# The gated merge of a hybrid decoder layer: from SBUF tiles to the PSUM banks of the products

## The chip, the cores and the metric

The kernel runs on one core of one Trainium2 chip. A core has five engines that work beside each other, each through its own queue in order: TensorE (PE in the profile, with its weight loads as PEld), VectorE (DVE), ScalarE (ACT), GpSimd (POOL) and SyncE (SP, which here issues most of the DMAs). They wait for each other by semaphores. Matrix products are written into PSUM, a small memory of eight banks; everything else lies in SBUF. The metric is the device time of one execution in microseconds (us), as the median of several runs. An execution with the hardware profiler gives the trace.

## The reference, cut to what matters

One inference step of a decoder layer for 512 prompt tokens and 8 x 4 decode tokens, 544 tokens in all, in fp32. Two attention branches run on the same normalised input: branch A, a sparse attention over the 256 best keys, and branch B, a stick-breaking attention. Each branch's output (512 wide) is projected to 1024 channels, the two are merged by sigmoid gates, and an output projection and a residual follow, then a SwiGLU FFN:

```python
gates = jax.nn.sigmoid(p[7]).reshape(b, t, 2, D_MODEL)
...
merged = gates[:, :, 0] * (o_a @ w_br_a) + gates[:, :, 1] * (o_b @ w_br_b)
return merged @ w_o
...
hp = hp + _mixers(...)
hp = hp + _ffn(_rmsnorm(hp, norm_ffn[layer]), w_ffn_gate[layer], w_ffn_up[layer], w_ffn_down[layer])
```

## The kernel before

Everything is computed transposed: channels lie on the 128 partitions, the 544 tokens along the free axis. A token axis is worked in two halves of 256 and 288 tokens (`halves`), because a PSUM bank holds 512 fp32 numbers per partition. A product of 1024 output channels is eight blocks m of 128 channels.

To keep fp32 accuracy in a faster number format (fp32r), every operand is split into a high and a low part, and a product is the sum of three matmuls (high weight by high data, low by high, high by low). The weights' parts are made on the way: class `Weights` loads a block by DMA from SP (`wst`, line 106), ACT copies the high part (`wh`, line 116), and POOL subtracts to get the low part in two instructions (`wl`, line 119). `W.take()` hands out the next block and prepares the blocks ahead. The inner loop of all such products is `pieces` (line 464): for each half it takes the next PSUM bank of a cycle and runs 3 matmuls for each of the nk slices of 128 input channels.

The banks have names: `mm` and `z` (one bank each), `acc`, `tp` and `ts` (two each), together eight. From here on the products go round the four banks `mm, z, acc, acc` (`banks`, line 454), one pair for each block m. The two `ts` banks serve the attention; after it nothing uses them until the FFN opens a new PSUM pool.

The place of the change is the merge, lines 1395 to 1411, between attention and output projection:

- `hT` (SBUF) holds the products of branch B. Five blocks were computed earlier and come back by DMA from DRAM (line 1402); the last three are computed here (lines 1396 to 1400).
- For each block m, two gate tiles `t` and `g` (tag `gt`, 8 buffers) are loaded by SP (line 1391) and put through a sigmoid by ACT (line 1392). POOL multiplies g into `hT` (line 1405).
- PE computes the block of branch A, 12 matmuls for each half (nk is 4). For each half DVE multiplies the bank by the gate t into SBUF (line 1407), adds `hT` (line 1408), ACT copies the result as the high part `mh` (line 1409), and DVE subtracts to get the low part `ml` (line 1410). `mh` and `ml` are the input of the output projection with `w_o`, eight blocks of 2 x 24 matmuls, whose results get the residual from transposed pieces of x (`xe`, line 1425, transposed by PE at line 414).

The instructions of each engine's queue are not in the order of the code. The framework schedules them by its own model of time over the whole program, so an edit in one place can move instructions elsewhere; it also puts in the semaphores, and lets a buffer be written again when its last reader is done.

Of the kernel before, what the change touches and what calls it, by code (L numbers as in the profile page):

```python
# [15 lines left out]
AF = mybir.ActivationFunctionType  # L16
# [245 lines left out]
def hybrid_step(ctx: ExitStack, tc: tile.TileContext, x_prompt, x_sample, cache_kv_a, cache_k_idx, cache_kv_b,  # L262
                page_table, w_in, w_br_a, w_br_b, w_o, norm_attn, norm_ffn, w_gate, w_up, w_down, norm_final,
                c_ident, c_rope, c_masks, y_p, y_s, kva_p, kidx_p, kvb_p, kva_s, kidx_s, kvb_s):
    nc = tc.nc
    S = lambda t: t.bitcast(F32)

    def opened(name, bufs=1, **kw):
        st = ExitStack()
        return st.enter_context(tc.tile_pool(name=name, bufs=bufs, reuse_waits="tile", **kw)), st  # L270
# [113 lines left out]
        nc.gpsimd.indirect_dma_start(out=dst, out_offset=None, in_=src,  # L384
                                     in_offset=bass.IndirectOffsetOnAxis(ap=rowid[:, n:n + 1], axis=0))

    V = {"wide": True}
    V["psum"], psum_end = opened("pmm", space=PSUM)

    def bank(tag, bufs):  # L390
        return V["psum"].tile([P, 512], F32, tag=tag, name=tag, bufs=bufs)

    mm = lambda: bank("mm", 1)
    zb = lambda: bank("z", 1)
    acc = lambda: bank("acc", 2)
    lat = lambda: bank("tp", 2)
    lts = lambda: bank("ts", 2)
# [7 lines left out]
    halves = [slice(0, 2 * P), slice(2 * P, TOK)]  # L405
# [45 lines left out]
    nc.vector.tensor_scalar(rowid, prow[:, :NSEQ], masks[:, 2 * P + 3 * NS:2 * P + 3 * NS + 1], None, op0=OP.add)  # L451
    xp_end.close()

    banks = cycle([mm, zb, acc, acc])


    def pieces(w, a, nk, m=P):

        (wh, wl), (ah, al) = w, a
        for f, hs in enumerate(halves):  # L460
            ps = (next(banks) if V["wide"] else mm)()[:m, :hs.stop - hs.start]
            for k in range(nk):
                for p, (ww, aa) in enumerate(((wh, ah), (wl, ah), (wh, al))):
                    nc.tensor.matmul(ps, ww[:, k, :m], aa[:, k, hs],  # L464
                                     start=(k == 0 and p == 0), stop=(k == nk - 1 and p == 2))
                yield None
            yield hs, ps

    def product(w, a, nk, m=P):
        return (part for part in pieces(w, a, nk, m) if part)  # L470
# [19 lines left out]
    def row(name, shape=(P, TOK), dt=F32):  # L490

        pool, bufs = V.get("rows", (rp if name == "y" else rr, (2, 2, 2, 1)))
        return pool.tile(list(shape), dt, tag="row" + name, name="row" + name, bufs=bufs["ywhl".index(name)])
# [10 lines left out]
    def rope(m=P, scale=1.0, also=None):  # L504
# [12 lines left out]
        nc.vector.tensor_mul(y[:m], y[:m], cosT[:m])  # L517
        (nc.vector if V["wide"] else nc.gpsimd).tensor_mul(w[:m], w[:m], sinT[:m])
        nc.vector.tensor_add(y[:m], y[:m], w[:m])
# [115 lines left out]
    def dense_idx():  # L635
        ip = V["ip"]
        qs, qbi, kinew, khh, kll, wiT, wtok, wrow = V["idx"]
# [652 lines left out]
    def branch_product(b):  # L1290
        return product(W.take(), place(b), 4)
# [77 lines left out]
    rp_end.close()  # L1369
    wk_end.close()  # L1370

    V["wide"] = True

    late, late_end = opened("late")
    hT = late.tile([P, KD, TOK], F32, name="hT")
# [8 lines left out]
    mh = ep.tile([P, KD, TOK], F32R, name="mh")  # L1384
    ml = ep.tile([P, KD, TOK], F32R, name="ml")
# [3 lines left out]
    def gate(m, b):  # L1389
        t = gp.tile([P, TOK], F32, tag="gt", name="gt", bufs=8)  # L1390
        nc.sync.dma_start(t, gate_d[:, 2 * m + b, :])
        nc.scalar.activation(t, t, AF.Sigmoid)
        return t
# [9 lines left out]
    for m in range(KD):  # L1403
        t, g = gate(m, 0), gate(m, 1)
        nc.gpsimd.tensor_mul(hT[:, m, :], g, hT[:, m, :])
        for hs, ps in branch_product(0):
            nc.vector.tensor_mul(t[:, hs], ps, t[:, hs])  # L1407
            nc.vector.tensor_add(t[:, hs], t[:, hs], hT[:, m, hs])
            nc.scalar.activation(mh[:, m, hs], t[:, hs], AF.Copy)
            nc.vector.tensor_sub(ml[:, m, hs], t[:, hs], S(mh[:, m, hs]))  # L1410
    W.extra, W.ahead = None, 1
    gp_end.close()
    xk_end.close()
# [41 lines left out]
    for hs in hv:  # L1455
        ps = lat()[:, :HN]
# [61 lines left out]
    x_parts("T4", t4)  # L1518
    psum_end.close()
    V["psum"], psum_end = opened("pff", space=PSUM)  # L1520
    tp2_end.close()
    xu_end.close()
    hp_end.close()
# [16 lines left out]
    for j in range(1, KF // 2):  # L1540
        banks2, kept = {}, {}
        for name in Pairs.REST if j > 1 else Pairs.FIRST:
# [4 lines left out]
            ps = banks2[b][:, :, :HN]  # L1547
# [107 lines left out]
                nc.sync.dma_start(y_s.rearrange("n t d -> (n t) d"), yt[:NS, i, :])  # L1655

    for m in range(KD):
        pss = [next(banks)()[:, :hs.stop - hs.start] for hs in halves]
        for ks in DOWN[0]:
            w = W.take()  # L1660
            for f, hs in enumerate(halves):
                down(pss[f], w, ks, hs)
        for f, hs in enumerate(halves):
            nc.vector.tensor_add(hT[:, m, hs], pss[f], hT[:, m, hs])
    act_parts(KF)
    for m in range(KD):
        pss = [next(banks)()[:, :hs.stop - hs.start] for hs in halves]
        if m < KD - 1:
            for ks in DOWN[1]:
                w = W.take()  # L1670
                for f in range(2):
                    down(pss[f], w, ks, halves[f])
            for f in range(2):
                rows_of(m, f, pss[f])
        else:
            ws = [W.take(), W.take()]
            for w, ks in zip(ws, DOWN[1]):
                down(pss[1], w, ks, halves[1])
            down(pss[0], ws[0], DOWN[1][0], halves[0])
            rows_done(1, rows_of(m, 1, pss[1]))  # L1680
            down(pss[0], ws[1], DOWN[1][1], halves[0])
            rows_done(0, rows_of(m, 0, pss[0]))
# [32 lines left out]
```

## Time and profile before

| | us |
|---|---|
| median of 3 runs | 1070.34 (1068.96 to 1074.01) |
| the profiled execution | 1067.42 |
| its span, first to last instruction | 1065.6 |

| engine | busy share of the span |
|---|---|
| PE | 92% |
| DVE | 70% |
| ACT | 50% |
| POOL | 44% |

The profile page gives shares over the whole span. The kernel has stages with different limits, so the page is only a start: the trace is asked for windows of time (busy time of each engine in each), for the instructions of one engine in order of time, and for groups of like instructions. In the windows table the numbers after each engine are its busy microseconds and, in brackets, its instructions; then come the granted TensorE clock as a share of full speed, the share of time that the DMA engines were busy, and GB/s. Matmuls overlap: one is shown as 0.28 us long, and the next starts 0.12 us after it.

### The profile page before, as it was taken

How to read it: one execution, taken by the hardware profiler on the slowest of the kernel's cores; microseconds unless marked ns; L12 is line 12 of the kernel's file. 1: busy time of each engine (PE TensorE's matmuls, PEld its weight loads, DVE VectorE, ACT ScalarE, POOL GpSimd, SP SyncE). 2: the span in 40 equal slices, each digit the busy share in tenths (PEclk: the TensorE clock that was granted, in tenths of full speed). 3: DMA queues.
4: the chain of work that ended last, by engine and by line, in shares of the span. 5: the costliest groups of instructions: out<-in, count | busy, mean ns of one | idle time of the engine just before them, and what ended most of it. 6: DMA issues, size and time to landing. Idle time of an engine off the chain costs nothing.

```text
span 1065.6 us, 20642 instructions
## 1 busy us (share of the span) xinstructions
PE 984.7 (92%) x7446; PEld 931.0 (87%) x7446; DVE 740.7 (70%) x1441; ACT 531.2 (50%) x1020; POOL 469.9 (44%) x413
## 2 busy tenths in 40 slices
PE   6899998787989996999999799979999999999995
PEld 5899998776669996888888799979999999999995
DVE  4468995798997786578784976787787876513233
ACT  6234535574556564677785544534444444423223
POOL 4555545226763236652635834411323232545441
PEclk9999999998999998999998999989999999999998
DMA  9775547886767765864525663223432341223222
GB/s 269 181 205 169 152 121 228 250 253 174 228 209 242 223 188 165 256 218 144 193 72 181 201 179 90 71 71 89 119 100 83 97 119 43 75 88 90 83 82 85
DMA packets 184704, 162.15 MB, mean 152 GB/s; under 512 B 13338, under 2 KB 148058, under 8 KB 183578
## 3 DMA queue, kind: packets, MB, share of 16 engines
q1 hardware_dynamic: 176410, 140.00, 45.5%
q0 software_dynamic: 1872, 10.75, 2.9%
q10 hardware_dynamic: 6320, 10.08, 2.9%
q8 instruction: 59, 0.97, 0.4%
q14 instruction: 43, 0.35, 0.1%
HBM read 133.37 MB, written 22.01 MB: 146 GB/s over the span
## 4 chain that ended last, share of the span: by engine, by line
PE 52%; DVE 11%; issue 7%; POOL 5%; DMA 4%; ACT 2%; SPq 1%; ACTq 0%; DVEq 0%; POOLq 0%
PE mm L464 8%; PE ffB L1553 8%; PE acc L1607 6%; PE ffC L1553 5%; PE ffA L1553 5%; POOL wl L119 4%; PE z L1607 3%; PE mm L1607 3%; PE acc L1021 2%; PE ts L992 2%; PE acc L1089 2%; DVE g L909 1%; DMA vb<-in_cache_kv_b 1%; PE tp L825 1%; PE tp L838 1%
## 5 line engine op out<-in xcount | busy, mean ns | idle before, releaser
L119 POOL TENSOR_TENSOR wl<-wst,wh 128x512 fp32r<-128x512 f32 (+2 forms) x198 | 228.8, 1177 | 193.8 <-ACT wh L116 193.8
L464 PE MATMUL mm<-xh,wh 128*128 128x256 f32 (+2 forms) x484 | 145.7, 301 | 9.3 <-ACT rowy L500 5.5
L464 PE MATMUL mm<-xh,wl 128*128 128x256 f32 (+2 forms) x484 | 141.6, 293 | 2.4 <-POOL wl L119 2.4
L464 PE MATMUL mm<-xl,wh 128*128 128x256 f32 (+2 forms) x484 | 142.5, 294 | 0.0
L116 ACT ACTIVATE wh<-wst 128x1024 fp32r<-128x1024 f32 (+3 forms) x99 | 88.6, 895 | 103.0 <-PE z L1607 42.1
L227 POOL TENSOR_TENSOR wl<-wst,wh 128x512 fp32r<-128x512 f32 x40 | 59.9, 1519 | 164.4 <-ACT wh L224 164.4
L464 PEld LDWEIGHTS mm<-xh,wh 128*128 128x128 f32 (+1 forms) x484 | 93.1, 192 | 21.0 <-issue 7.3
L464 PEld LDWEIGHTS mm<-xh,wl 128*128 128x128 f32 (+1 forms) x484 | 93.1, 192 | 3.4 <-POOL wl L119 2.6
L464 PEld LDWEIGHTS mm<-xl,wh 128*128 128x128 f32 (+1 forms) x484 | 93.0, 192 | 0.5
L224 ACT ACTIVATE wh<-ws 128x1024 fp32r<-128x1024 f32 x40 | 42.4, 1061 | 68.5 <-PE ffC L1553 36.1
L1607 PE MATMUL acc<-actp,wh 128*128 128x256 f32 (+1 forms) x352 | 68.1, 289 | 0.0
L910 POOL TENSOR_TENSOR b<-b,g 128x127 f32<-128x127 f32 (+3 forms) x32 | 28.4, 887 | 82.8 <-DVE g L909 43.0
L229 DVE TENSOR_TENSOR wl<-ws,wh 128x1024 fp32r<-128x1024 f32 x40 | 52.1, 1301 | 6.0 <-ACT wh L224 6.0
L1607 PEld LDWEIGHTS acc<-actp,wh 128*128 128x128 f32 x352 | 55.4, 188 | 0.1
L998 DVE TENSOR_TENSOR kl<-ts,kh 128x512 fp32r<-128x512 f32 x64 | 43.4, 686 | 16.2 <-ACT kh L997 15.5
L464 PE MATMUL acc<-xh,wh 128*128 128x256 f32 (+1 forms) x176 | 51.3, 293 | 3.1 <-DVE gt L1407 2.7
L464 PE MATMUL acc<-xh,wl 128*128 128x288 f32 (+1 forms) x176 | 51.4, 293 | 0.0
L464 PE MATMUL acc<-xl,wh 128*128 128x288 f32 (+1 forms) x176 | 51.0, 291 | 0.0
L1607 PE MATMUL acc<-actp,wl 128*128 128x256 f32 (+1 forms) x176 | 49.9, 288 | 1.2 <-POOL wl L119 1.2
L997 ACT ACTIVATE kh<-ts 128x512 fp32r<-128x512 f32 x64 | 38.0, 602 | 23.9 <-PE ts L992 20.1
L1083 POOL TENSOR_TENSOR vl<-vb,vh 128x512 fp32r<-128x512 f32 x24 | 36.6, 1529 | 28.0 <-ACT vh L1082 24.9
L1082 ACT ACTIVATE vh<-vb 128x512 fp32r<-128x512 f32 x64 | 38.4, 626 | 20.6 <-DMA vb<-in_cache_kv_b 13.0
(438 smaller groups left out, 3433.7 us busy)
## 6 DMA issues: line engine op xcount, KB each, us to landing
wst<-in_w_in SPq DMA_DIRECT2D x38, 512.0 KB, 4.3
kb<-in_cache_kv_b SPq DMA_DIRECT2D x64, 256.0 KB, 4.6
vb<-in_cache_kv_b SPq DMA_DIRECT2D x64, 256.0 KB, 4.0
wst<-in_w_ffn_gate SPq DMA_DIRECT2D x40, 256.0 KB, 3.0
wst<-in_w_ffn_up SPq DMA_DIRECT2D x40, 256.0 KB, 3.4
wst<-in_w_ffn_down SPq DMA_DIRECT2D x16, 384.0 KB, 3.6
wst<-in_w_ffn_down SPq DMA_DIRECT2D x16, 320.0 KB, 3.2
gate_d<-rowy ACTq DMA_DIRECT2D x16, 272.0 KB, 4.2
```

Of the source, the lines that this page charges most:

```text
L116: self.nc.scalar.activation(h, st, AF.Copy)
L119: self.nc.gpsimd.tensor_sub(l[:, k], st[:, k], h[:, k].bitcast(F32))
L224: self.nc.scalar.activation(h, src, AF.Copy)
L227: self.nc.gpsimd.tensor_sub(l[:, g], src[:, g], h[:, g].bitcast(F32))
L229: self.nc.vector.tensor_sub(l, src, h.bitcast(F32))
L464: nc.tensor.matmul(ps, ww[:, k, :m], aa[:, k, hs], start=(k == 0 and p == 0), stop=(k == nk - 1 and p == 2))
L997: nc.scalar.activation(kh[:, :, :2 * P], tpv, AF.Copy)
L998: nc.vector.tensor_sub(kl[:, :, :2 * P], tpv, S(kh[:, :, :2 * P]))
L1082: nc.scalar.activation(vh, raw, AF.Copy)
L1083: (nc.vector if pg % 3 else nc.gpsimd).tensor_sub(vl, raw, S(vh))
L1553: nc.tensor.matmul(ps[:, g], ww[:, g, k, :], aa[:, k, :], start=(first and k == 0 and p == 0), stop=(k == 3 and p == 2), skip_group_check= ...
L1607: nc.tensor.matmul(ps, ww[:, k - ks[0], :], aa[:, hs], start=(k in (DOWN[0][0][0], DOWN[1][0][0]) and p == 0), stop=(k + 1 in (DOWN[0][1][ ...
```

## The change

The merge of a half is done in the PSUM bank that its product stands in. Line 1407 multiplies the bank by t and writes the bank, line 1408 adds `hT` to the bank and writes the bank, line 1409 reads the high part from the bank and line 1410 the low part. The gate tile t is only read. A bank is therefore held until line 1410 has read it, where before it was free after line 1407.

From the merge on, the products go round six banks, `mm, z, acc, acc, ts, ts`. The cycle now lies in `V["banks"]`; it is set back to the four banks when the FFN's PSUM pool opens.

```diff
-    V = {"wide": True}
+    V = {"wide": True, "banks": cycle([])}
...
-    banks = cycle([mm, zb, acc, acc])
+    V["banks"], many = cycle([mm, zb, acc, acc]), cycle([mm, zb, acc, acc, lts, lts])
...
-            ps = (next(banks) if V["wide"] else mm)()[:m, :hs.stop - hs.start]
+            ps = (next(V["banks"]) if V["wide"] else mm)()[:m, :hs.stop - hs.start]
...
-    V["wide"] = True
+    V["wide"], V["banks"] = True, many
...
         nc.gpsimd.tensor_mul(hT[:, m, :], g, hT[:, m, :])
         for hs, ps in branch_product(0):
-            nc.vector.tensor_mul(t[:, hs], ps, t[:, hs])
-            nc.vector.tensor_add(t[:, hs], t[:, hs], hT[:, m, hs])
-            nc.scalar.activation(mh[:, m, hs], t[:, hs], AF.Copy)
-            nc.vector.tensor_sub(ml[:, m, hs], t[:, hs], S(mh[:, m, hs]))
+            nc.vector.tensor_mul(ps, ps, t[:, hs])
+            nc.vector.tensor_add(ps, ps, hT[:, m, hs])
+            nc.scalar.activation(mh[:, m, hs], ps, AF.Copy)
+            nc.vector.tensor_sub(ml[:, m, hs], ps, S(mh[:, m, hs]))
...
     V["psum"], psum_end = opened("pff", space=PSUM)
+    V["banks"] = cycle([mm, zb, acc, acc])
...
-        pss = [next(banks)()[:, :hs.stop - hs.start] for hs in halves]
+        pss = [next(V["banks"])()[:, :hs.stop - hs.start] for hs in halves]
```

The schedule moves with it. DVE's queue near the end of the merge, before: the instructions on block 6 (banks `mm` and `z`) stand between those of the blocks beside it.

```order
L1407 TENSOR_TENSOR gt<-mm,gt 128x256
L1410 TENSOR_TENSOR ml<-gt,mh 128x256
L1407 TENSOR_TENSOR gt<-z,gt 128x288
L1410 TENSOR_TENSOR ml<-gt,mh 128x288
L1408 TENSOR_TENSOR gt<-gt,hT 128x256
L1408 TENSOR_TENSOR gt<-gt,hT 128x288
L1410 TENSOR_TENSOR ml<-gt,mh 128x256
```

The two rows of line 1410 that stand between the two multiplications belong to block 5. The same place in the changed kernel:

```order
L1407 TENSOR_TENSOR mm<-mm,gt 128x256
L1407 TENSOR_TENSOR z<-z,gt 128x288
L1408 TENSOR_TENSOR mm<-mm,hT 128x256
L1408 TENSOR_TENSOR z<-z,hT 128x288
L1410 TENSOR_TENSOR ml<-mm,mh 128x256
L1410 TENSOR_TENSOR ml<-z,mh 128x288
```

All six instructions of the block now stand together, and each has a bank as an operand.

POOL's queue in the middle of the merge: line 1405 is the product of gate and `hT` of a block, line 119 the low part of a weight block of branch A (two instructions for a block).

```order
 L1405 TENSOR_TENSOR hT<-gt,hT 128x544
 L119 TENSOR_TENSOR wl<-wst,wh 128x256 x2
-L1405 TENSOR_TENSOR hT<-gt,hT 128x544 x2
-L119 TENSOR_TENSOR wl<-wst,wh 128x256 x2
-L1405 TENSOR_TENSOR hT<-gt,hT 128x544
-L119 TENSOR_TENSOR wl<-wst,wh 128x256 x2
+L1405 TENSOR_TENSOR hT<-gt,hT 128x544 x3
+L119 TENSOR_TENSOR wl<-wst,wh 128x256 x4
 L1405 TENSOR_TENSOR hT<-gt,hT 128x544
 L119 TENSOR_TENSOR wl<-wst,wh 128x256 x2
```

Three products with `hT` (blocks 2, 3 and 4) now come before the low parts of the weights of blocks 5 and 6, where before the weights of block 5 came after two.

PE's queue at the start of the output projection, before, where the first transposes of `xe` come:

```order
L464 MATMUL acc<-ml,wh 128x256
L464 MATMUL acc<-mh,wl 128x288
L414 MATMUL tp<-ident,xe 128x128 x4
L414 MATMUL tp<-ident,xe 128x32
L464 MATMUL acc<-ml,wh 128x288
```

And in the changed kernel:

```order
L464 MATMUL ts<-ml,wh 128x288
L414 MATMUL tp<-ident,xe 128x128 x4
L464 MATMUL ts<-mh,wh 128x288
L464 MATMUL ts<-mh,wl 128x288
L464 MATMUL ts<-ml,wh 128x288
```

Before, 74 matmuls of the projection stand ahead of the first transpose, in the changed kernel 47.

The order of the last part of the attention, ahead of the merge, moves too: PE's twelve matmuls for a branch B block in bank `mm`, cut in three before by attention work, stand together, and those for the next half in bank `z` come five matmuls of the attention's values later.

## Rows read from the trace of the kernel before

**Rows 1.** Windows of the core, by stage; the first line names the columns.
```profile
core 0: us, PE busy (x) PEld busy (x) DVE busy (x) ACT busy (x) POOL busy (x), PEclk, DMA share, GB/s
562.00:570.00 8.00, 7.76 (x42) 6.87 (x41) 2.39 (x8) 2.33 (x5) 3.12 (x3) 0.57 0.62 207
...
575.00:590.00 15.00, 15.00 (x123) 15.00 (x122) 8.42 (x15) 10.77 (x20) 11.59 (x13) 1.00 0.71 211
590.00:616.00 26.00, 18.85 (x137) 17.16 (x136) 25.45 (x36) 13.14 (x25) 19.08 (x16) 1.00 0.72 209
616.00:690.00 74.00, 74.00 (x573) 72.02 (x572) 50.61 (x69) 37.21 (x57) 31.33 (x21) 1.00 0.39 110
```

**Rows 2.** PE's timeline: start, us, instruction, idle time before it and releaser.
```profile
594.61 0.40 PE L464 MATMUL acc<-xh,wh 128*128 128x288 f32 x1 [1.59 <-DVE gt L1407]
...
603.95 0.40 PE L464 MATMUL acc<-xh,wh 128*128 128x288 f32 x1 [1.07 <-DVE gt L1407]
...
614.25 0.40 PE L464 MATMUL acc<-mh,wh 128*128 128x288 f32 x1 [1.79 <-DVE gt L1407]
```

**Rows 3.** Windows of PE alone, from the merge's first product to the first transpose.
```profile
574.78:590.00 15.22, 15.22 (x125) 1.00 0.70 208
590.00:620.05 30.05, 22.90 (x170) 1.00 0.75 216
```

**Rows 4.** DVE's groups by shape, 575 to 616: count | busy, mean ns | idle before.
```profile
L1408 DVE TENSOR_TENSOR gt<-gt,hT 128x256 f32<-128x256 f32 x8 | 8.0, 1003 | 0.6 <-POOL hT L1405 0.6
L1408 DVE TENSOR_TENSOR gt<-gt,hT 128x288 f32<-128x288 f32 x8 | 7.4, 921 | 0.0
L1410 DVE TENSOR_TENSOR ml<-gt,mh 128x256 fp32r<-128x256 f32 x8 | 7.4, 920 | 0.0
L1410 DVE TENSOR_TENSOR ml<-gt,mh 128x288 fp32r<-128x288 f32 x8 | 6.6, 820 | 0.2 <-ACT mh L1409 0.2
...
L1407 DVE TENSOR_TENSOR gt<-acc,gt 128x288 f32<-128x288 f32 x4 | 1.8, 444 | 0.0
...
L1407 DVE TENSOR_TENSOR gt<-acc,gt 128x256 f32<-128x256 f32 x4 | 1.7, 414 | 1.0 <-PE acc L464 1.0
```

**Rows 5.** DVE's timeline near the merge's end.
```profile
612.35 1.48 DVE L1408 TENSOR_TENSOR gt<-gt,hT 128x256 f32<-128x256 f32 x1
...
614.23 0.46 DVE L1408 TENSOR_TENSOR gt<-gt,hT 128x288 f32<-128x288 f32 x1
```

**Rows 6.** POOL's timeline in the merge.
```profile
574.93 2.84 POOL L119 TENSOR_TENSOR wl<-wst,wh 128x256 fp32r<-128x256 f32 x4 [1.59 <-ACT wh L116]
581.18 1.37 POOL L1405 TENSOR_TENSOR hT<-gt,hT 128x544 f32<-128x544 f32 x1 [3.41 <-ACT gt L1392]
...
610.82 2.73 POOL L119 TENSOR_TENSOR wl<-wst,wh 128x512 fp32r<-128x512 f32 x2 [0.35 <-ACT wh L116]
```

**Rows 7.** POOL's groups by shape, 575 to 616.
```profile
L119 POOL TENSOR_TENSOR wl<-wst,wh 128x256 fp32r<-128x256 f32 x16 | 13.3, 859 | 1.6 <-ACT wh L116 1.6
L1405 POOL TENSOR_TENSOR hT<-gt,hT 128x544 f32<-128x544 f32 x8 | 12.2, 1530 | 5.4 <-ACT gt L1392 5.4
```

**Rows 8.** ACT's groups by shape, whole span.
```profile
L816 ACT ACTIVATE tp<-tp 128x256 f32<-128x256 f32 x8 | 2.9, 366 | 5.2 <-PE tp L815 5.1
...
L1400 ACT ACTIVATE hT<-acc 128x256 f32<-128x256 f32 x2 | 0.8, 384 | 2.6 <-PE acc L464 2.6
```

**Rows 9.** Waits, 575 to 616: us in total, times, longest.
```profile
ACT mh L1409 <- DVE gt L1408: 14.5, 14, 3.2
```

**Rows 10.** SP's timeline at the merge's end, issues of DMAs.
```profile
607.00 0.37 SPq L186 DMA_DIRECT2D wst<-in_w_ffn_gate  x1
...
611.86 0.69 SPq L1425 DMA_DIRECT2D xe<-in_x_prompt  x1
```

**Rows 11.** The loads of tile xe, all of the program.
```profile
DMA to landing us min/median/max: 2.8/3.0/4.6
```

**Rows 12.** DVE's timeline, first instruction after the FFN's norm.
```profile
673.95 1.64 DVE L1475 TENSOR_TENSOR hg<-hg,rst 128x1088 f32<-128x1088 f32 x1 [3.72 <-ACT rst L1460]
```

More of the change, by code (lines that the diff above doesn't have):

```diff
@@ L1666, in hybrid_step @@
     for m in range(KD):
-        pss = [next(banks)()[:, :hs.stop - hs.start] for hs in halves]
+        pss = [next(V["banks"])()[:, :hs.stop - hs.start] for hs in halves]
         if m < KD - 1:
```

## The prediction

> **What bounds the kernel now.** I read the windows by stage first, because the page's 92% for PE is a mean over stages. The windows [rows 1] show three kinds of stretch around the change. From 575 to 590 PE is busy all the time. From 590 to 616 DVE is busy 25.45 of 26 us and PE only 18.85: here DVE is the bound, and PE is idle for 26.00 - 18.85 = 7.15 us. From 616 to 690 PE is full again. The granted clock is 1.00 in all three, so PE's loss in the middle stretch is waiting and nothing else. The timeline of PE names what it waits for: it has eight gaps from 594.61 to 614.25, and the three longest [rows 2] all end with line 1407 on DVE, which is what gives a bank back. The other five are shorter; two of these wait for the split of w_o's first block on ACT and POOL, and one for line 1409.
>
> The idle time undercounts the loss, because the first matmul after a gap starts the pipeline anew. Counting matmuls gives it better [rows 3]. In the full stretch 125 matmuls take 15.22 us, 0.1218 us each. The 170 matmuls from 590.00 to 620.05 would take 170 x 0.1218 = 20.7 us at that pace; they took 30.05. PE lost 9.3 us between the merge and the first transpose. That is the most that this change can return at its own place.
>
> Why DVE is slow there stands in its groups by shape [rows 4]. Line 1407, with one operand in a bank, takes 414 ns for 256 columns and 444 ns for 288. Lines 1408 and 1410, with both operands in SBUF and as many elements, take 820 to 1003 ns in the mean. Two neighbouring instructions show that this is no property of the operation [rows 5]: at 612.35 line 1408 took 1.48 us while POOL worked from 610.82 to 613.55 [rows 6], and at 614.23, with POOL idle, line 1408 took 0.46 us on 288 columns. So an instruction with two SBUF inputs waits for POOL's, and line 1407 does not.
>
> **The change, part by part.**
>
> DVE. 48 instructions stay 48 (3 lines, 2 halves, 8 blocks), but all now have one input in a bank. Before they cost 8.0 + 7.4 + 7.4 + 6.6 for lines 1408 and 1410 and about 7.0 for line 1407 (16 times 0.414 to 0.444), 36.4 us [rows 4]; durations overlap a little, so they fit in some 34. After, at line 1407's durations: 3 x (0.414 + 0.444) = 2.57 us a block, 20.6 us for eight. PE needs 24 x 0.1218 = 2.92 us a block, 23.4 us for eight. DVE falls below PE, and PE is the bound of the merge again.
>
> No row shows DVE writing into a bank, so this is bounded from both sides. From below, 0.41 us: no less, since elements and passes are the same. From above, 1.48 us, the dearest row of the kind [rows 5]. The nearest row is of ACT: it copies 256 columns from a bank into the same bank in 366 ns, and from a bank to SBUF in 384 ns [rows 8], so a result in the bank costs nothing more there. I take 0.41 and 0.44 us and keep the upper end for the rival below. The Trainium skill ("SBUF — State Buffer", Who interferes with whom) says that a VectorE instruction with at most one SBUF input, outside the two-port modes, does not contend with GpSimd; by it the sum for DVE is 20.6 us as well, and line 1407's rows agree as far as a result in SBUF goes.
>
> ACT. The 16 copies of line 1409 now read a bank; the rows of lines 816 and 1400 [rows 8] stand at 366 and 384 ns, no dearer than a copy from SBUF. ACT's time there is mostly waiting: 14.5 us for line 1408 in 14 waits [rows 9]. The split of w_o's first weight blocks stands behind these copies in ACT's queue, so it moves forward with them.
>
> The banks. A bank was held until line 1407; now it is held until line 1410, which needs POOL's product with hT (line 1405) and ACT's copy. That is the added wait: behind it on PE stand all later products. Per block the chain after PE's last matmul is multiply, add, copy, subtract, about 4 x 0.43 = 1.7 us, in DVE's queue some 2.6 us. Six banks are three pairs, so a pair is needed again 2 x 2.92 = 5.8 us after its product ends. This covers the chain with 3.2 us to spare, while with four banks only 0.3 us would be left. For the early blocks POOL's product must come within that spare time; its first ends at 582.55 [rows 6], and the pair of block 0, whose product ends near 577.8, is wanted again by block 3, after the last branch B block and blocks 1 and 2, near 586.5. The tightest reuse is that of block 2's pair by block 5, since POOL's product for block 2 now comes late in its queue; I cost it at 0.2 us.
>
> POOL is late next. Undisturbed its split of a block costs 2 x 0.71 (four took 2.84) and its product with hT 1.37 [rows 6]; in the merge the means are 859 and 1530 ns [rows 7], beside DVE's instructions with two SBUF inputs. From 581.18 on it has 8 products and 12 halves of a split left: 8 x 1.37 + 12 x 0.71 = 19.5 us, until 600.7. PE would finish the merge's products at 574.78 + 216 x 0.1218 = 601.1 (nine blocks of 24: the eight of branch A and the last of branch B), and then wants w_o's first split. Its first half takes 2.73 / 2 = 1.37 us [rows 6], until 602.1, against two matmuls that can go without it: PE waits 0.8 us, and starting anew costs 0.26 (the 9.3 - 7.15 us of above over eight gaps). I take 1.0. In the order POOL now does three products with hT ahead of the weights of blocks 5 and 6; the first half of block 5's weights then comes at 581.18 + 5 x 1.37 + 7 x 0.71 = 593.0, block 5 starts on PE at 574.78 + 6 x 24 x 0.1218 = 592.3 and can do two matmuls without it: 0.4 us, with the new start 0.7; the bank wait of 0.2 falls into the same gap, and I take 0.7 for both.
>
> The transposes of xe stand 47 matmuls after the start of the projection instead of 74, that is at 601.1 + 1.0 + 5.7 = 607.8. Their load on SP comes after the first FFN weights, which wait for the last product: before they were issued at 607.00 and xe at 611.86 [rows 10], with five other issues between; now only one more FFN load stands between, about 1 us of issue in all, so xe goes out near 602.5 and lands 2.8 to 4.6 us later [rows 11], by 607.1. I take 0.1 us.
>
> Downstream nothing gives the time back. From 616 to 690 PE is full [rows 1], and each weight block follows PE's release of the one before. Then DVE is the bound for a while, but that stretch begins with line 1475, which waits 3.72 us for ACT's norm [rows 12], which waits for PE; it moves as a whole. So the sum is 9.3 - 1.0 - 0.7 - 0.1 = 7.5 us. The profiled execution took 1067.42 us (span 1065.6 and 1.8 around it): 1059.9 after. The median of the runs shown is 1070.34, 2.9 us above it; taking the 7.5 us from the median gives 1062.8, and this I predict.
>
> Ahead of the merge the schedule of the attention's last 20 us moves a little. PE's work is the same; at 562 to 570 the granted clock is 0.57 [rows 1], close to the lower of its levels (1.2 of 2.4 GHz), which costs 8 x 0.43 = 3.4 us. If the moved order shifts that stretch, it can give back or cost up to that; I take zero and keep 3.4 us for both ends.
>
> **The rivals.**
>
> POOL becomes the bound. If POOL stays as slow as now, it needs 8 x 1.53 + 12 x 0.859 = 22.5 us from 581.18, until 603.7, and w_o's first half comes at 605.1: PE waits 4.0 us there and not 0.8. The gain is 4.3 us, 1066.0. For it: POOL is busy 19.08 of 26 us [rows 1] and is my next-late engine by a margin of 0.4 us. Against it: what slows POOL are DVE's instructions with two SBUF inputs, and none are left in the merge.
>
> The gain stays but PE's clock or the moved attention takes some back. PE now runs without a break in the merge, cycling six banks; ahead of it the dip of 562 to 570 may come a second time or last twice as long: 7.5 - 3.4 = 4.1 us, 1066.2. For it: a dip stands there already. Against it: with four banks and eight gaps the clock stayed at 1.00 from 590 to 616 [rows 1]. The Trainium skill ("TensorE: Matmul & The Clock Gate", A second HAM failure mode: psum-queue depth-cycling) warns that cycling through PSUM banks leaves small idle times between groups in which the clock is throttled again and again; by it the merge itself would run partly at half clock, 1066.2 if for as long as that dip, and the trace disagrees so far.
>
> DVE is slower in the bank (the case on the other side). If a result in a bank costs DVE as much as the rows with two SBUF inputs, the 32 instructions of lines 1407 and 1408 take 1.00 us [rows 4] to 1.48 us [rows 5] each, and line 1410 its 6.9 us in all: 38.9 to 54.3 us, against 36.4 of durations now. PE then stalls for banks as before, for 2.5 to 17.9 us more; in the middle, 10.2 us, 1080.5. It decides from (36.4 - 6.9) / 32 = 0.92 us an instruction; up to (23.4 - 6.9) / 32 = 0.52 us PE hides it. For it: no row shows DVE writing PSUM. Against it: ACT's row in the same bank [rows 8].
>
> That the change does not do what it says (too few banks, an operand still in SBUF) I leave out: the order shows `ts` in the cycle and a bank in each of the 48 instructions.
>
> **How the numbers follow.** The forecast, 1062.8 with 1061 to 1065 as its own range (between all 9.3 us and somewhat under 6), gets 0.62. POOL as the bound gets 0.13, the loss in clock or attention 0.14, the slower case 0.09, and 0.02 is for more than 9.3 us (the dip shortened, 1059). A measurement of this kernel can tell about 0.5%, 5.3 us, from no change. The forecast lies beyond it in nearly all its range (0.58), the 0.02 with the dip shortened does too, and of the middle cases a small part (0.06): faster 0.66. The rest of the middle cases and a little of the forecast is within 0.5%: 0.25. Slower is 0.09. The range goes from 1057.5, the forecast with the dip shortened and a part of the spread of the runs, to 1069.5, which takes in both middle cases with that spread and leaves out the slower case.
>
> **What would show it.** In the profile after: lines 1407, 1408 and 1410 all at 0.41 to 0.46 us with POOL busy; POOL's line 119 near 0.71 and line 1405 near 1.37; DVE no longer full between 590 and 610 and PE full there; 24 matmuls every 2.9 us for all eight blocks; the last product of the merge near 601 to 602, the first transpose near 608 and not 620, and from there on the same times as before, earlier by about 7.5 us. The first doubt falls on POOL if PE's gaps end with line 119, on the banks if they end with line 1410. The prediction is wrong if lines 1407 and 1408 take more than 0.5 us, or if the stretch up to 575 has moved by more than 2 us.

## The result, and the profile after

The changed kernel takes 1063.69 us (median of 12 runs, 1058.57 to 1065.72); the kernel before, on the same chips, 1069.68 us (12 runs, 1065.46 to 1074.01). The ratio is 0.9945 with a 95% interval of 0.9931 to 0.996: 6.0 us faster, 0.55%. The prediction was 1062.8 us.

The windows by stage of the changed kernel, at the times of [rows 1], with the same columns (start and end, length, then busy time and instructions of each engine, granted clock, DMA share, GB/s):

```profile
core 0: us, PE busy (x) PEld busy (x) DVE busy (x) ACT busy (x) POOL busy (x), PEclk, DMA share, GB/s
562.00:570.00 8.00, 6.95 (x48) 6.09 (x49) 5.64 (x13) 5.95 (x15) 6.19 (x7) 0.81 0.16 46
575.00:590.00 15.00, 15.00 (x107) 14.96 (x108) 5.62 (x16) 9.57 (x19) 7.95 (x11) 0.89 0.67 223
590.00:616.00 26.00, 25.81 (x208) 25.56 (x207) 18.06 (x45) 17.37 (x35) 21.33 (x21) 1.00 0.88 246
616.00:690.00 74.00, 73.26 (x566) 71.31 (x565) 50.94 (x67) 36.46 (x55) 33.86 (x21) 1.00 0.37 105
```

From 590 to 616 PE is now busy 25.81 of 26 us (before 18.85) and does 208 matmuls (before 137); DVE is busy 18.06 us (before 25.45). The bound of the merge went from DVE back to PE. POOL, which I had feared as the next bound, is busy a little longer there (21.33 us, before 19.08), with more done in it: 21 instructions, before 16.

DVE's groups by shape, 575 to 616, the counterpart of [rows 4] (one bank's name for each shape; the other names differ by at most 8 ns):

```profile
L1407 DVE TENSOR_TENSOR acc<-acc,gt 128x288 f32<-128x288 f32 x3 | 1.4, 463 | 0.5 <-PE acc L464 0.5
L1408 DVE TENSOR_TENSOR acc<-acc,hT 128x288 f32<-128x288 f32 x3 | 1.4, 460 | 0.0
L1410 DVE TENSOR_TENSOR ml<-acc,mh 128x288 fp32r<-128x288 f32 x3 | 1.3, 448 | 0.0
...
L1407 DVE TENSOR_TENSOR acc<-acc,gt 128x256 f32<-128x256 f32 x3 | 1.3, 426 | 0.9 <-ACT gt L1392 0.9
L1408 DVE TENSOR_TENSOR acc<-acc,hT 128x256 f32<-128x256 f32 x3 | 1.3, 426 | 0.1
L1410 DVE TENSOR_TENSOR ml<-acc,mh 128x256 fp32r<-128x256 f32 x3 | 1.3, 419 | 0.5 <-ACT mh L1409 0.5
```

All 48 instructions stand between 0.41 and 0.47 us. Lines 1408 and 1410, which took 820 to 1003 ns, take half of that. ACT's waits for line 1408, 14.5 us before [rows 9], are down to two (us in total, times, longest):

```profile
ACT mh L1409 <- DVE ts L1408: 0.7, 1, 0.7
...
ACT mh L1409 <- DVE acc L1408: 0.4, 1, 0.4
```

POOL's groups in the same window are the counterpart of [rows 7]:

```profile
L119 POOL TENSOR_TENSOR wl<-wst,wh 128x256 fp32r<-128x256 f32 x16 | 11.3, 736 | 1.6 <-ACT wh L116 1.6
L1405 POOL TENSOR_TENSOR hT<-gt,hT 128x544 f32<-128x544 f32 x8 | 10.8, 1365 | 5.0 <-ACT gt L1392 5.0
```

The split fell from 859 to 736 ns and the product with hT from 1530 to 1365 ns. The collision cost both sides, and both got the time back.

PE's timeline after (start, us, instruction, idle time before it and its releaser). Between the merge's first matmul and the sums of squares at line 1457 only two rows have an idle time, where before there were eight gaps:

```profile
613.94 0.24 PE L414 MATMUL tp<-ident,xe 32*128 32x32 f32 x1 [0.19 <-DMA xe<-in_x_sample]
...
621.74 0.41 PE L414 MATMUL tp<-ident,xe 128*128 128x128 f32 x2 [0.74 <-DMA xe<-in_x_prompt]
```

These two are new: transposes of xe that wait for their loads. To compare local stretches I take the time from the merge's first matmul of `mm` to the first matmul of line 1457, which holds the same 690 matmuls in each kernel (a record or two may be missing). First the kernel before, then the changed kernel:

```profile
574.79:671.77 96.98, 89.83 (x690) 86.47 (x689) 68.43 (x101) 50.19 (x87) 54.48 (x44) 1.00 0.54 157
```

```profile
578.04:668.09 90.05, 89.12 (x689) 87.24 (x689) 53.50 (x101) 49.19 (x86) 51.23 (x44) 0.99 0.59 170
```

The stretch is 6.93 us shorter. PE's idle time in it fell from 96.98 - 89.83 = 7.15 us to 0.93 us, and the rest, 0.71 us, is in its busy time. From the merge's first matmul to the end of the span it is 1065.6 - 574.79 = 490.81 against 1062.8 - 578.04 = 484.76 us: 6.05 us, and the medians differ by 6.0. As far as one execution of each kernel can tell, the gain arises in the merge, and 0.9 us of it is lost after line 1457. That the two numbers agree so closely is luck: in the repeat below the same difference is 6.8 us.

### The profile page after: what moved, and what is told of

Same layout as the page of the kernel before. It is cut to its first block, busy times and chain, and to the rows that moved or that the text cites. A ratio compares the mean times of both kernels' runs of the same rounds, so it can differ in the third digit from the quotient of the medians.

```text
span 1062.8 us, 20643 instructions
## 1 busy us (share of the span) xinstructions
PE 991.5 (93%) x7446; PEld 938.1 (88%) x7446; DVE 725.5 (68%) x1441; ACT 530.5 (50%) x1020; POOL 465.2 (44%) x413
## 4 chain that ended last, share of the span: by engine, by line
PE 54%; DVE 12%; issue 6%; DMA 4%; POOL 4%; ACT 2%; SPq 1%; ACTq 0%; DVEq 0%; POOLq 0%
PE mm L464 9%; PE ffB L1554 8%; PE acc L1608 6%; PE ffC L1554 5%; PE ffA L1554 5%; POOL wl L119 3%; PE z L1608 3%; PE mm L1608 3%; PE ts L992 2%; PE acc L1021 2%; PE acc L1089 2%; DVE g L909 1%; PE tp L838 1%; DVE vl L1083 1%; DMA kb<-in_cache_kv_b 1%
## 5 line engine op out<-in xcount | busy, mean ns | idle before, releaser
L119 POOL TENSOR_TENSOR wl<-wst,wh 128x512 fp32r<-128x512 f32 (+2 forms) x198 | 225.5, 1161 | 187.9 <-ACT wh L116 185.3
L464 PEld LDWEIGHTS mm<-xh,wl 128*128 128x128 f32 (+1 forms) x480 | 94.6, 197 | 0.8
L992 PE MATMUL ts<-ident,kb 128*128 128x128 f32 x256 | 41.8, 281 | 6.7 <-DMA kb<-in_cache_kv_b 5.0
L464 PE MATMUL acc<-xh,wl 128*128 128x256 f32 (+1 forms) x160 | 46.5, 292 | 0.0
L464 PE MATMUL acc<-xl,wh 128*128 128x256 f32 (+1 forms) x160 | 46.1, 290 | 0.0
```

The source lines that it names most:

```text
L119: self.nc.gpsimd.tensor_sub(l[:, k], st[:, k], h[:, k].bitcast(F32))
L464: nc.tensor.matmul(ps, ww[:, k, :m], aa[:, k, hs], start=(k == 0 and p == 0), stop=(k == nk - 1 and p == 2))
L992: nc.tensor.transpose(tp[:, (2 * j + pg) * P:(2 * j + pg + 1) * P], V["kp"][pg][:, (2 * jj + j) * P:(2 * jj + j + 1) * P], ident)
```

## The experiments

All ratios are to the kernel before, run on the same chip. "The stretch" is the one just defined. It is taken from one execution each, and where PE's clock falls to half for some 2 us inside it, it is about 1.1 us longer; I say where that is so (see "The clock" below). In the execution of the kernel before it is not.

**Six banks, merge in SBUF.** The change's first part alone.

```diff
-    banks = cycle([mm, zb, acc, acc])
+    V["banks"], many = cycle([mm, zb, acc, acc]), cycle([mm, zb, acc, acc, lts, lts])
...
-    V["wide"] = True
+    V["wide"], V["banks"] = True, many
```

> Six banks in turn, but the merge in SBUF as in the kernel before. Measured by the stretch from the merge's first matmul on block 0 to the first matmul of the FFN's norm (line 1457): 97.0 us before, 90.1 in the changed kernel. Theory A (the gain is that no DVE instruction of the merge has two SBUF inputs beside POOL's): lines 1408 and 1410 stay at 0.8 to 1.0 us in the mean, DVE stays full for some 25 us, and only the waits for a bank at the very end go: stretch 95 to 97, time 0 to 2 us under the kernel before. Theory B (the gain is the two more banks, which let PE run ahead): stretch 90 to 91, 5 to 7 us faster.

Measured: 1069.77 us, ratio 0.9996 (0.998 to 1.0012), stretch 577.62 to 674.70, 97.1 us. One of DVE's slow groups in this kernel (the other three are at 865 to 895 ns), and gaps of PE:

```profile
L1408 DVE TENSOR_TENSOR gt<-gt,hT 128x288 f32<-128x288 f32 x8 | 7.4, 920 | 0.0
```

```profile
598.59 0.40 PE L464 MATMUL z<-xh,wh 128*128 128x288 f32 x1 [1.33 <-DVE gt L1407]
603.05 0.52 PE L464 MATMUL acc<-xh,wh 128*128 128x256 f32 x2 [1.32 <-ACT wh L116]
...
611.24 0.52 PE L464 MATMUL ts<-mh,wh 128*128 128x256 f32 x2 [2.18 <-ACT wh L116]
```

Only one gap still ends with line 1407: two more banks let PE run ahead. But DVE is as slow as before, so PE meets it a block later: at ACT's split of the weights, which stands in ACT's queue behind copies that wait for DVE (13.6 us in 11 waits for line 1408). The waits have other names and nearly the same sum: PE's idle time in the stretch is 6.6 us, before 7.15. This execution has a half-clock stretch in its merge (granted clock 0.50 from 578 to 580); without it the stretch would be near 96 us. So banks alone are worth about 1 us in the stretch, and the measured times show nothing of it.

**Merge in the banks, four banks.** The other part alone: the changed kernel with the cycle of the kernel before.

```diff
-    V["banks"], many = cycle([mm, zb, acc, acc]), cycle([mm, zb, acc, acc, lts, lts])
+    banks = cycle([mm, zb, acc, acc])
...
-    V["wide"], V["banks"] = True, many
+    V["wide"] = True
```

> The merge in the PSUM banks, but four banks in turn as before. Theory A: DVE's 48 instructions at 0.41 to 0.47 us, DVE no longer full, POOL's rows at 0.71 to 0.74 and 1.37; PE now waits for banks that are held until line 1410, by the estimate of the prediction (2.6 us of chain in 2.92) a little for each block, more where POOL's product with hT is late: stretch 91 to 94, time 3 to 6 us under the kernel before. Theory B: without the banks nothing is gained, and since banks are held longer the stretch is 97 or more.

Measured: 1064.09 us, ratio 0.9954 (0.9934 to 0.9973), stretch 576.68 to 668.50, 91.8 us. All 48 DVE instructions are at 417 to 467 ns and POOL at 731 and 1357 ns, as in the changed kernel. PE's gaps in the merge:

```profile
587.16 0.38 PE L464 MATMUL mm<-xh,wh 128*128 128x256 f32 x1 [0.22 <-DVE ml L1410]
591.30 0.39 PE L464 MATMUL acc<-xh,wh 128*128 128x256 f32 x1 [0.88 <-DVE ml L1410]
```

This is the wait that the prediction expected of four banks ("only 0.3 us would be left"): the bank is held until line 1410, and the second gap costs 0.88 us. With six banks both are gone. Behind the merge PE waits another 0.88 us in two gaps for DVE's line 1430, about what the changed kernel loses to the loads of xe, and a half-clock stretch lies in both executions (here 0.50 from 576 to 578), so the two can be compared: the two extra banks give 91.8 - 90.05 = 1.8 us in the stretch, of which 1.1 us are the two gaps shown. In the ratios the two intervals overlap, so this part shows in the trace and is too small for the measured times.

**Only lines 1407 and 1408 read the bank.** Four banks; line 1408 reads the bank and writes SBUF, so line 1410 has two SBUF inputs again.

```diff
-            nc.vector.tensor_add(ps, ps, hT[:, m, hs])
-            nc.scalar.activation(mh[:, m, hs], ps, AF.Copy)
-            nc.vector.tensor_sub(ml[:, m, hs], ps, S(mh[:, m, hs]))
+            nc.vector.tensor_add(t[:, hs], ps, hT[:, m, hs])
+            nc.scalar.activation(mh[:, m, hs], t[:, hs], AF.Copy)
+            nc.vector.tensor_sub(ml[:, m, hs], t[:, hs], S(mh[:, m, hs]))
```

> Four banks; line 1407 writes the bank, line 1408 reads the bank and writes SBUF, lines 1409 and 1410 read SBUF as before, so that only line 1410 has two SBUF inputs and the bank is free after line 1408. Theory A: line 1408 falls to 0.42 to 0.47 us, line 1410 stays at 0.8 to 0.95; DVE's work is 13.7 + 14 = 28 us against 36 before and 23.4 that PE needs: about half of the gain, stretch 92.5 to 95, 2 to 4 us faster. Theory B: 97, no gain.

Measured: 1066.24 us, ratio 0.9972 (0.9948 to 0.9996), stretch 575.35 to 670.0, 94.6 us. DVE and POOL by shape, 575 to 620:

```profile
L1410 DVE TENSOR_TENSOR ml<-gt,mh 128x288 fp32r<-128x288 f32 x8 | 9.2, 1148 | 0.0
L1410 DVE TENSOR_TENSOR ml<-gt,mh 128x256 fp32r<-128x256 f32 x8 | 7.2, 897 | 1.4 <-ACT mh L1409 1.4
...
L1408 DVE TENSOR_TENSOR gt<-acc,hT 128x288 f32<-128x288 f32 x4 | 1.8, 452 | 0.1
...
L1408 DVE TENSOR_TENSOR gt<-acc,hT 128x256 f32<-128x256 f32 x4 | 1.6, 412 | 0.0
```

```profile
L119 POOL TENSOR_TENSOR wl<-wst,wh 128x256 fp32r<-128x256 f32 x16 | 12.4, 803 | 1.6 <-ACT wh L116 1.6
L1405 POOL TENSOR_TENSOR hT<-gt,hT 128x544 f32<-128x544 f32 x8 | 11.4, 1433 | 5.8 <-ACT gt L1392 5.8
```

The line that reads a bank is fast, the line that has two SBUF inputs is slow, in one kernel and with the same elements: the operand decides, not the line. POOL stands between its values with none of the lines slow (731) and with two (859 before). The one line that still collides is dearer than before for 288 columns (1148 against 820 ns) and as dear for 256 (897 against 920), so of two slow lines one does not simply cost half. PE still waits 4.3 us in four gaps, all for the bank that line 1408 gives back. A half-clock stretch falls into it too (0.50 from 608 to 610); without that, near 93.5 us, about half of the gain is there, as expected.

**Without POOL's product of gate and hT.** The kernel before with line 1405 taken out. Branch B then goes into the merge without its gate; the work of the other engines stays.

```diff
-        nc.gpsimd.tensor_mul(hT[:, m, :], g, hT[:, m, :])
```

> The kernel before with POOL's product of gate g and hT (line 1405) left out, so the output lacks the gate of branch B. Merge in SBUF, four banks. Theory A: POOL's work in the merge falls from 25 to 11 to 13 us, so lines 1408 and 1410 meet it half as often: means of 0.6 to 0.75 us instead of 0.82 to 1.0, stretch 92 to 95, 2 to 5 us faster. Theory B (banks): 97, no gain.

Measured: 1067.36 us, ratio 0.9981 (0.9963 to 0.9999). Line numbers are one lower here; DVE's add and subtraction, 575 to 620:

```profile
L1409 DVE TENSOR_TENSOR ml<-gt,mh 128x288 fp32r<-128x288 f32 x8 | 6.9, 860 | 1.0 <-ACT mh L1408 1.0
L1407 DVE TENSOR_TENSOR gt<-gt,hT 128x256 f32<-128x256 f32 x8 | 5.6, 704 | 0.1
L1409 DVE TENSOR_TENSOR ml<-gt,mh 128x256 fp32r<-128x256 f32 x8 | 4.4, 547 | 0.6 <-ACT mh L1408 0.6
L1407 DVE TENSOR_TENSOR gt<-gt,hT 128x288 f32<-128x288 f32 x8 | 4.2, 519 | 0.0
```

```profile
626.67 0.54 PE L414 MATMUL tp<-ident,xe 128*128 128x128 f32 x2 [2.36 <-DVE hT L1429]
```

With half of POOL's work gone the same DVE instructions, still in SBUF, cost 519 to 860 ns instead of 820 to 1003. That is the other half of the proof: DVE was slow because POOL read at the same time. PE has a single gap left between 575 and 620, 0.83 us for POOL's split. The stretch is 93.3 us (578.73 to 672.02), 3.7 us shorter than before, within what was expected, although 2.36 us in it go into a later wait of the transposes of xe for a copy on DVE (the row above) and the clock is at 0.50 from 627 to 630. Why that copy is late in this kernel I did not follow further. Of the 3.7 us some 2 show in the measured time, whose interval reaches from 0.1 to 4 us.

**The changed kernel again,** unchanged, for a second profile and ratio.

> The changed kernel as it is, once more, for a second profile and a second ratio on the same chip as the run with the earlier xe loads. Theory A: no gap of TensorE in the merge, again a wait of the xe transposes for a DMA of about 1 us in all, stretch from the merge's first matmul to the first matmul of line 1457 between 88.5 and 91 us, according to where the half-clock stretch near 565 to 582 us falls; ratio 0.9931 to 0.996 as before. Rival (the 0.5% was one chip's or one execution's): ratio within 0.2% of 1, or the stretch above 93 us.

Measured: 1063.79 us, ratio 0.9937 (0.9915 to 0.996). Its stretch, and the only two gaps in it:

```profile
578.49:667.90 89.41, 87.97 (x690) 86.08 (x689) 53.43 (x101) 49.20 (x87) 51.99 (x44) 1.00 0.59 171
```

```profile
613.24 0.24 PE L414 MATMUL tp<-ident,xe 32*128 32x32 f32 x1 [0.20 <-DMA xe<-in_x_sample]
621.51 0.41 PE L414 MATMUL tp<-ident,xe 128*128 128x128 f32 x2 [1.25 <-DMA xe<-in_x_prompt]
```

The gain stands. The wait for xe comes back in the same place (1.45 us in all), so it belongs to the kernel and not to one execution. In this execution no half-clock stretch fell into the merge, and PE's busy time is 1.15 us less than in the first profile (87.97 against 89.12).

**xe loaded earlier.** The changed kernel, with the first two loads of xe issued at blocks 6 and 7 of the merge; the gate tiles have one buffer less for it.

```diff
+    xe_pool, xe_end = opened("xe")
...
-        t = gp.tile([P, TOK], F32, tag="gt", name="gt", bufs=8)
+        t = gp.tile([P, TOK], F32, tag="gt", name="gt", bufs=7)
...
+        if m > KD - 3:
+            early.append(xe_load(m - KD + 2))
...
+        xe = early[m] if m < 2 else xe_load(m)
```

> The changed kernel, with the first two loads of xe (the inputs of the block-6 transposes that w_o's stage carries) issued inside the merge loop, at its blocks 6 and 7, instead of after it; the pool of xe stands ahead of that of the gates, which gives one buffer less to gt. In the changed kernel TensorE waits 0.19 us at 613.94 and 0.74 us at 621.74 for a DMA of xe, and the stretch from the merge's first matmul to the first matmul of line 1457 is 90.05 us. Theory A (the xe loads, now late, are the mis-sized term of the sum: about 1 us): no wait of a transpose for a DMA of xe is left, the stretch is 88.5 to 89.5 us, and the time is about 1 us under the changed kernel's, near 1062.5, ratio to the kernel before 0.993 to 0.995. Rival (the loads are only the last to arrive; the copies of the transposed tiles or the clock end later anyway): the waits move to another releaser, the stretch stays at 90 us or above, ratio 0.9945 to 0.997.

Measured: 1061.11 us, ratio 0.9919 (0.9897 to 0.9942). The stretch:

```profile
574.24:662.00 87.76, 87.76 (x691) 86.10 (x690) 53.22 (x101) 49.33 (x87) 50.31 (x44) 1.00 0.60 174
```

PE is busy in every one of its 87.76 us; the first transpose of xe is now at 589.2, inside the merge. With it the third load moves too: it goes out at 590.0, when the first block's transposes have given its buffer back. Against the repeat above, which had no half-clock stretch either, that is 1.65 us less: the 1.45 us of waiting and 0.2 us. The stretch and the ratio are a little better than theory A had them, but theory and rival differ in whether the waits vanish, and they do. In the ratio this version and the repeat, on the same chip, still overlap.

**The kernel before with xe loaded earlier.** The same edit without the change.

> The kernel before (merge in SBUF, four banks), with the two first loads of xe issued at blocks 6 and 7 of the merge and one gt buffer less, as in the run with the earlier xe loads. In the kernel before no transpose of xe waits for a DMA, TensorE waits 9.3 us in the merge for the gate's instruction, and the stretch from the merge's first matmul to the first matmul of line 1457 is 96.98 us. Theory A (the xe loads became a cost only because the merge no longer holds TensorE up; the merge's waits stay): gaps of TensorE in the merge of 6 to 9 us remain, stretch 94.5 to 97.5 us (some transposes can now fill a gap), ratio 0.9965 to 1.0005. Rival (most of what the earlier loads give is from the order of the transposes inside the merge, with the merge in SBUF too): stretch 92 to 94.5 us, ratio 0.994 to 0.9965.

Measured: 1067.46 us, ratio 0.9985 (0.9973 to 0.9997), stretch 573.01 to 667.60, 94.6 us. Three of PE's five gaps:

```profile
593.87 0.40 PE L464 MATMUL acc<-xh,wh 128*128 128x288 f32 x1 [0.97 <-DVE gt L1419]
602.00 0.38 PE L464 MATMUL acc<-xh,wh 128*128 128x256 f32 x1 [1.57 <-DVE gt L1419]
...
614.43 0.40 PE L464 MATMUL z<-mh,wh 128*128 128x288 f32 x1 [0.77 <-ACT mh L1421]
```

This one comes out between the two theories. The merge's waits stay and the ratio is the first one's, but PE's idle time is 94.59 - 90.07 = 4.52 us, less than the 6 to 9 expected. The stretch stands at the border of the two, and a half-clock stretch at its start (0.50 from 572 to 574) adds about 1 us to it. About 2 us of time are gained without the change. A likely reason is that the transposes, which now stand inside the merge, do some of their work while PE would wait for banks; I did not separate it from the loads. So the earlier loads do more than repair what the change broke.

**xe loaded earlier, again.**

> The run with the earlier xe loads once more, for its ratio: it was 0.9919 (0.9897 to 0.9942), with a stretch of 87.76 us from the merge's first matmul to the sums of squares after w_o, all of it busy on TensorE. Theory A: again no wait for xe, stretch 87.5 to 89.5 us (a half-clock stretch inside it costs up to 1.6 us), ratio 0.990 to 0.9945. Rival (the first ratio was by chance, the loads give nothing beyond the changed kernel): ratio 0.9945 to 0.997.

Measured: 1060.35 us, ratio 0.9909 (0.989 to 0.9928). No wait in the stretch; a half-clock stretch lies in it this time, and it is longer by 1.08 us:

```profile
578.46:667.30 88.84, 88.84 (x689) 87.18 (x689) 53.10 (x101) 49.24 (x86) 50.61 (x44) 0.99 0.60 172
```

The 12 runs of this version have a mean of 1060.6 us, the 18 runs of the changed kernel 1063.4: 2.8 us less, with an interval of about 1.0 to 4.6 from their spreads (2.5 and 2.1 us); the runs are from more than one chip. By this it is faster than both kernels of this study.

## Why the prediction was right

**The bound and its cause.** Right. DVE was slow because its instructions with two SBUF inputs met POOL's, and a bank operand takes them out of the collision. Three experiments show it: bank operands alone bring the gain (0.9954), more banks alone bring nothing that the times show (0.9996), and less of POOL's work makes the untouched DVE instructions faster. The one execution of the kernel before says the same: of the 32 instructions of lines 1408 and 1410, the 8 that met no instruction of POOL took 406 to 459 ns, and the 18 that had POOL busy beside them for over 95% of their time took 1035 ns in the mean. Line 1407, with POOL as busy beside it seven times, took 409 to 448 ns. The Trainium skill ("SBUF — State Buffer", Who interferes with whom) states that a VectorE instruction with two SBUF inputs contends with a GpSimd instruction that reads SBUF, and one with at most one, outside the two-port modes, does not; the 452 and 1148 ns of two lines of one kernel, both for 288 columns, agree.

**DVE's price in the bank.** I took 0.41 and 0.44 us; the trace has 0.42 to 0.43 and 0.45 to 0.46. The case on the other side, 0.92 us or more, is refuted: a result in a bank costs up to 19 ns.

**The 9.3 us that PE lost.** They came back nearly whole. The repeat shows it best, since its merge has no half-clock stretch: the stretch is 96.98 - 89.41 = 7.57 us shorter, and 1.45 us of waiting for xe is still in it. That makes 9.0 us returned; of these 7.15 were idle time and 1.9 us are PE's busy time (89.83 against 87.97), most of it the new starts after gaps, which counting matmuls had caught and the idle time had not.

**POOL late twice, 1.0 and 0.7 us.** Neither occurred, the first by a narrow margin. The changed kernel's rows of POOL's first split of w_o, and of PE's first matmuls on w_o, the third of which needs it:

```profile
604.64 1.29 POOL L119 TENSOR_TENSOR wl<-wst,wh 128x512 fp32r<-128x512 f32 x1
```

```profile
606.16 0.41 PE L464 MATMUL ts<-mh,wh 128*128 128x256 f32 x2
606.41 0.28 PE L464 MATMUL ts<-mh,wl 128*128 128x256 f32 x1
```

The half is ready at 605.93, 0.48 us before PE wants it. Counted from the merge's first matmul POOL's half came 27.9 us after it, in the repeat 26.7 (603.93 + 1.27 - 578.49), where I had 27.3; but PE got to w_o after 28.1 us, in the repeat 27.0 (605.45 - 578.49), where I had 26.3. The pace of 0.1218 us was a miscount. A window counts every matmul that runs in it, and two of the 125 had begun before 574.78:

```profile
574.53 0.29 PE L464 MATMUL acc<-xh,wl 128*128 128x288 f32 x1
574.66 0.29 PE L464 MATMUL acc<-xl,wh 128*128 128x288 f32 x1
```

The 123 that begin in it start 0.1244 us apart; in the repeat one of 256 columns starts every 0.117 us and one of 288 every 0.132, and the merge has as many of each, 0.125 in the mean. Over 216 matmuls that is 0.7 us, nearly all of the wait of 0.8. The loss of 9.3 us stands by luck, since the 170 of the other window holds three too many as well: 167 x 0.1244 = 20.8. Block 5 did not wait for its weights or its bank either; by the right pace it starts 0.4 us later than I had it, as much as that wait. POOL as the bound, the rival at 1066.0, is refuted by 736 and 1365 ns.

**The loads of xe, 0.1 us.** The mis-sized term: it cost 0.9 and 1.45 us in the two profiles. I had worked out only the first load, to go out 27.7 us after the merge's start and to land at most 4.6 us later. SP's timeline of the changed kernel:

```profile
606.22 0.37 SPq L186 DMA_DIRECT2D wst<-in_w_ffn_gate  x1
606.64 0.50 SPq L186 DMA_DIRECT2D wst<-in_w_ffn_up  x1
607.24 0.46 SPq L1425 DMA_DIRECT2D xe<-in_x_prompt  x1
...
608.29 1.13 SPq L1426 DMA_DIRECT2D xe<-in_x_sample  x1
...
614.61 0.84 SPq L186 DMA_DIRECT2D wst<-in_w_ffn_up  x1
615.54 0.77 SPq L1425 DMA_DIRECT2D xe<-in_x_prompt  x1
```

The first load goes out at 607.24, 29.2 us after the merge's start, behind two loads of FFN weights, as I had it, and 1.5 us late because PE came to w_o later; PE has no idle time before its transposes at 612.04. The samples' load behind it, at 608.29, costs 0.19 us. The larger wait, 0.74 us at 621.74 and 1.25 in the repeat, is for the third block's load, the one at 615.54, which I had not worked out at all. Tile xe has two buffers, so this load needs the transposes of the first block, which end at 614.18; SP then still issues FFN weights, and the load goes out 1.4 us later. Before, the third load went out as soon as the first block's transposes ended (620.12 + 0.77):

```profile
620.93 0.37 SPq L1425 DMA_DIRECT2D xe<-in_x_prompt  x1
```

The loads also take longer to land. For tile xe, the counterpart of [rows 11]:

```profile
DMA to landing us min/median/max: 2.6/3.8/6.1
```

The longest, 6.1 us, is the third block's load (615.54 to 621.60); before, it took 3.0. The DMAs moved 292 GB/s from 614 to 622 and, before, 148 from 620 to 628, which fits, though no run separates the traffic from the late issue. When a stretch ahead gets shorter, what is loaded at its end loses its cover, and the price has to be worked out for every load behind it and with the busier DMAs, not with the times of before.

**The clock.** I gave a loss in clock ahead of or in the merge its own rival, 3.4 us. In the first profile of the changed kernel a half-clock stretch lies inside the merge:

```profile
578.00:580.00 2.00, 2.00 (x11) 2.00 (x11) 0.46 (x1) 1.71 (x2) 2.00 (x4) 0.50 0.00 0
```

From 578 to 580 the granted clock is 0.50, 1.2 of 2.4 GHz, and PE does 11 matmuls where 17 of 256 columns would fit at 0.117 us. PE's busy time in the stretch is 1.15 us more than in the repeat. So a second dip did come, as this rival had it, but the two of this execution cost as much as the one before did: 0.72 from 566 to 572 and from 576 to 582, 12 x 0.28 = 3.4 us. And nothing ties it to the change: in the repeat it is over before the merge starts, in two executions of the version with the earlier loads it lies once ahead of the merge and once in it, and dips fall into the stretch of all five experiments without the change or with a part of it. From 590 to 616 the clock is 1.00 in the changed kernel, so going round six banks did not lower it.

**Downstream.** As predicted, the FFN's norm moved as a whole. DVE's first instruction after it still waits 3.7 us for ACT, as in [rows 12], 3.63 us earlier on the clock of the span and 6.9 us earlier counted from the merge's start:

```profile
670.32 1.64 DVE L1475 TENSOR_TENSOR hg<-hg,rst 128x1088 f32<-128x1088 f32 x1 [3.70 <-ACT rst L1460]
```

**"Wrong if the stretch up to 575 has moved by more than 2 us."** It has, by 3.25 us (578.04 against 574.79), and this test was a bad one. The version with the earlier loads, one and the same program, starts its merge at 574.24 in one execution and at 578.46 in another. Start times of one execution each say nothing about a change; differences inside an execution say more.

**The sum.** By the repeat 9.0 - 1.45 = 7.6 us in the stretch, where I had 7.5. That is luck in part: the two terms of POOL that did not come (1.7) make up for the larger one of xe (1.35) and the 0.3 that did not come back. Some 0.8 us of it is not there at the end (484.01 us from merge start to end against 490.81, so 6.8), and the medians differ by 6.0. What takes the 0.8 us after line 1457 stays open; in one profile of the version with the earlier loads it is not lost (393.8 us from line 1457 to the end, as before; the changed kernel 394.7, the other profile of the earlier loads 394.1).

## What to carry to other kernels

Where an engine's instructions cost twice what the same shape costs elsewhere in the trace, look for a neighbour on a shared path before counting work; an operand left in PSUM was most of the remedy here, and it sped up the neighbour too. Count a loss in instructions at full pace, not in idle time: the idle time here missed 1.9 of 9 us. Take the pace from starts, not from a window's count. When a stretch gets shorter, list the loads for use right behind it, also those that wait for a buffer, and price them with the DMA traffic of the shorter stretch.

## What the runs showed that I had not expected

- A DVE result written into the bank that it reads costs little, but not nothing: line 1407 takes 426 to 433 and 463 ns, against 414 and 444 with the result in SBUF [rows 4]; line 1408 takes 426 and 460 ns, against 412 and 452 where it reads a bank and writes SBUF.
- The collision is not shared out evenly: with one colliding line instead of two, that line rose from 820 to 1148 ns for 288 columns and stayed for 256 (920 and 897).
- Executions of one program differ by where the clock dips. Over the 18 runs of the changed kernel the span goes with the mean granted clock (0.967 to 0.981) at about 0.5 us for each 0.001, with a correlation of -0.87. With it goes most of the spread of some 7 us between runs.
